# One tile of gathered and one of turned rows for all fours of experts, weights in two more places, and evictions put between the matmuls that turn the rows

## The chip, the core and the metric

The kernel runs on one core of one Trainium2 chip. The metric is the device time of one execution in microseconds (us), the median of several runs. The profile is of one execution. Engines are named as in the profile: PE is TensorE, DVE VectorE, ACT ScalarE, POOL GpSimd, SP SyncE, which issues the loads of weights.

## What is computed

Two transformer blocks over 512 tokens of width 1024, in float32. The change touches the last part of the second block alone, a mixture of 32 experts in four groups. Each token goes to two experts of one group. What has to come out is this sum, kept here in its plainest form:

```python
for e in range(N_EXPERTS):                       # 32 experts, w_gate and w_up 1024x256, w_down 256x1024
    act = jax.nn.silu(hf @ w_gate[e]) * (hf @ w_up[e])
    y = y + combine[:, e:e + 1] * (act @ w_down[e])
x = x + gate2 * y
```

The weights of the experts are 32 x 3 x 1 MB; every one of them has to be read once.

## The kernel before

Before the experts, the kernel writes the 512 rows of the block's input to a DRAM tile `h_d` and to the output, works out each token's experts, and sorts the tokens by expert (lines 1880 to 2060). An expert has 32 or more places for rows. The experts are worked in eight **fours**: the 128 rows of a four are 4 x 32 places, and a second set of 128 (`r` = 0 and 1) takes what the experts with many tokens have over.

For each four `q`:

- `rows_in(q)` **gathers** 2 x 128 rows from `h_d` into a tile `gb`, by two indirect DMAs on POOL.
- `turn(q, r, banks)` **turns** 128 rows: eight matmuls against a scaled unit matrix (`norm_of`, tile `dg`) put the 1024 columns of the rows on the partitions, into two PSUM banks; eight evictions, alternately ACT and DVE, write `xT[:, r]`.
- Twelve **jobs** of 1 MB of weights each: eight (`k` = 0 to 7) for the gate and up products, four (`k` = 8 to 11) for the down product. A job is two half jobs (`r` = 0, 1) of four matmuls of 128x32 with 512 columns. For `r` = 1 the weights are first copied to a tile `wd` in another order (`deal`, line 2197; half of it on DVE, half on ACT).
- `acts` and `acts_T` (activation and its transposes, line 2170), `halves` (the down product's eviction, times the token's weight, into `yo`, line 2211), `add_rows` (two **scatters** on POOL that add the rows to the output in DRAM, line 2177).

The jobs run in a fixed order: the first four's eight gate and up jobs, then for each next four its eight and then the four down jobs of the four before it; at the end the last four's down jobs. Every engine works through its instructions in the order in which this code issues them. `beside(q, k)` issues what is put beside job `k`: the turns of four `q + 1` behind jobs 4 and 6 of four `q`, and the gathers of four `q + 2` behind job 6. Two tiles `gb` and two tiles `xT` are used in turn (`q % 2`).

Weights come through a ring of places, each 1 MB: 3 `wr`, 3 `wq`, 10 `wb`. `st.fill()` issues a load on SP as soon as the order of the program has a free place, and `st.free` hands a place back behind each job. `st.left` = `EARLY` = 3 says that the first three `wb` places that become free are not loaded again: the second `gb`, the second `xT` and `yo` take their room. From then on 13 places are in use.

While the tokens are being sorted, `keep_busy(n)` puts `n` filler matmuls (128x512, line 1880) into PE's order.

Of the kernel before, what the change touches and what calls it, by code (L numbers as in the profile page):

```python
# [15 lines left out]
AF = mybir.ActivationFunctionType  # L16
OP = mybir.AluOpType
# [3 lines left out]
D = 1024  # L21
# [15 lines left out]
NQ = NE // 4  # L37
# [4 lines left out]
MORE0, EARLY = 7, 3  # L42
# [316 lines left out]
def tile_kernel(ctx: ExitStack, tc: tile.TileContext, ws, ada, c_d, hT_d, cst_d, seq_d, bd_d, wr_d, pos_d, out):  # L359
    nc = tc.nc  # L360
    V, S, G, PE = nc.vector, nc.scalar, nc.gpsimd, nc.tensor
# [11 lines left out]
    bank = [psum.tile([128, 512], FT, name=f"bank{i}") for i in range(8)]  # L373
    B = lambda shape, dt=FT, name="b": bpool.tile(shape, dt, name=name, tag="B")
# [177 lines left out]
    st = Stream(order)  # L552
# [251 lines left out]
    p = unitA(v_h, v_l, two_banks)  # L804
# [3 lines left out]
    vm = mpool.tile([16, 128], FT, name="vm", tag="vm", bufs=1)  # L808
# [92 lines left out]
    vfm = mpool.tile([16, 512], FT, name="vfm", tag="vfm", bufs=1)  # L901
# [975 lines left out]
    def keep_busy(n):  # L1877

        for _ in range(n):
            PE.matmul(bank[1], lhsT=ident, rhs=io, start=True, stop=True)  # L1880

    gb, xT, yo = [], [], []

    def rows_place():
        gb.append(B([128, 2, D], name="gb"))
        G.memset(gb[-1], 0.0)
        xT.append(B([128, 2, 8, 128], name="xT"))

    rows_place()


    sc, used = [], [0]
# [50 lines left out]
    V.tensor_tensor(oh, io9[:, None, None, :].to_broadcast([128, 2, 4, 32]),  # L1943
                    ek[:, :, :, None].to_broadcast([128, 2, 4, 32]), op=OP.is_equal)
    V.tensor_add(cnt_h, oh[:, 0], oh[:, 1])
    keep_busy(9)

    pt, before, placed = bank[0][:, :32], *(bank[0][:, 32 + 128 * j:160 + 128 * j].rearrange("p (i e) -> p i e", i=4)
                                            for j in range(2))
# [4 lines left out]
        for i in (3, 2, 1):  # L1954
            PE.matmul(ps[:, 4 - i:], lhsT=every, rhs=cnt_h[:, :i], start=False, stop=i == 1 and ps is before)
    PE.matmul(placed, lhsT=every, rhs=first_4, start=False, stop=True)
    keep_busy(8)
    V.tensor_sub(ex, m2, m1)

    def over(x):  # L1960
# [59 lines left out]
        hot(k)  # L2020
    inv = bank[2][:, :16]
    by_slot(inv, ohb, lambda n: tk[:, n, 0])
    keep_busy(2)
    hidx = cpool.tile([128, 16], I32, name="hidx")
    r4s, w_s = (cpool.tile([128, 16], FT, name=n) for n in ("r4s", "w_s"))
    V.tensor_scalar(hidx, inv, float(NONE), None, op0=OP.add)
# [7 lines left out]

    def rows_in(q):
        for r in range(2):
            gather(gb[q % 2][:, r], hidx[:, 2 * q + r:2 * q + r + 1])

    rows_in(0)
    st.hold, st.queue = False, G  # L2040
# [102 lines left out]
    def norm_of(scale, tag):  # L2143
        d = mpool.tile([128, 128], FT, name="dg", tag=tag, bufs=1)
        V.tensor_scalar(d, ident, scale, None, op0=OP.mult)
        return d

    def turned(x, g, d, banks):

        for h, p in enumerate(banks):  # L2150
            for t in range(4):
                PE.matmul(p[:, 128 * t:128 * t + 128], lhsT=g[:, 512 * h + 128 * t:512 * h + 128 * t + 128], rhs=d,
                          start=True, stop=True)
            for t in range(4):
                n, s = 4 * h + t, p[:, 128 * t:128 * t + 128]
                if t % 2:
                    V.tensor_scalar(x[:, n], s, a1[:, 8 + n:9 + n], MOD(3, n), op0=OP.mult, op1=OP.add)
                else:
                    S.activation(x[:, n], s, AF.Identity, bias=MOD(3, n), scale=a1[:, 8 + n:9 + n])

    def act(p):
        a = mpool.tile([128, 256], FT, name="ea", tag="cbm")
# [13 lines left out]
    def scatter(y, idx):  # L2176
        return G.indirect_dma_start(out=out[0], out_offset=bass.IndirectOffsetOnAxis(ap=idx, axis=0), in_=y,  # L2177
                                    in_offset=None, bounds_check=SEQ - 1, oob_is_err=False, compute_op=OP.add)

    def turn(q, r, banks):  # L2180
        turned(xT[q % 2][:, r], gb[q % 2][:, r], norm_of(r4s[:, 2 * q + r:2 * q + r + 1], "vfm" if r else "vm"), banks)

    def lot_regs(q):
        return [vload(lot_i[0:1, 4 * q + j:4 * q + j + 1], 1536, [ET.DVE if j < 2 else ET.Activation]) for j in range(4)]
# [21 lines left out]
    def own(w):  # L2206
        return lambda j: w[:, 512 * j:512 * j + 512]

    def halves(q, h):
        for r in range(2):  # L2210
            V.scalar_tensor_tensor(yo[0][:, r, 512 * h:512 * h + 512], bank[4 + 2 * h + r], w_s[:, 2 * q + r:2 * q + r + 1],
                                   gate[h], op0=OP.mult, op1=OP.mult)

    def add_rows(q):
        last = scatters[-1:]
        scatters[:] = [scatter(yo[0][:, r], hidx[:, 2 * q + r:2 * q + r + 1]) for r in range(2)]
        if q == NQ - 1:

            tc.declare_no_dep(scatters[1].ins, scatters[0].ins, reason="no row of out in both")
            tc.add_manual_dep(scatters[1].ins, last[0].ins.name,  # L2220
                              mybir.DependencyInfo(mybir.DependencyClass.Sync, mybir.DependencyReason.DATA),
                              reason="rows of out added to before")

    a, aT, scatters = {}, {}, []

# [8 lines left out]
    def beside(q, k):  # L2234

        other = bank[2 - 2 * (q % 2):4 - 2 * (q % 2)]
        aside[0] = other[1]
        if q and k == 0:
            acts(q - 1)
        elif q and k == 2:  # L2240
            acts_T(q - 1)
        elif k in (4, 6) and q + 1 < NQ:
            turn(q + 1, k // 2 - 2, other)
            if k == 6 and q + 2 < NQ:
                rows_in(q + 2)
        if q == 0 and k == 2:
            rows_place()
            rows_in(1)
            yo.append(B([128, 2, D], name="yo"))
            later.add(slot_weights())  # L2250
        elif q == 1 and k == 3:
            later.finish()
            later.add(crowded())
        elif q > 1 and k in (5, 7):
            later.tick()

    st.fill()
    st.left = EARLY
    turn0 = [norm_of(r4s[:, r:r + 1], "vfm" if r else "vm") for r in range(2)]
    dealt[0] = deal(0)  # L2260
    turned(xT[0][:, 0], gb[0][:, 0], turn0[0], bank[2:4])
    for i, (q, n) in enumerate(jobs):
        if i + 1 < len(jobs):
            dealt[i + 1] = deal(i + 1)
        w, t = dealt.pop(i)
        k = n - n_dense - 12 * q
        for r in range(2):
            if i == 0 and r == 1:
                turned(xT[0][:, 1], gb[0][:, 1], turn0[1], bank[4:6])
            if k < 8:  # L2270
                ps, x = bank[2 * (q % 2) + r], lambda c: xT[q % 2][:, r, k, c]
                first, last = k == 0, k == 7
            else:
                ps, x = bank[4 + 2 * (k // 10) + r], lambda c: aT[q][r][:, k % 2, c]
                first, last = k % 2 == 0, k % 2 == 1
            product(ps, x, (lambda j: t[:, j]) if r else own(w), first, last)
        st.free(("w", n))
        w = t = None
        st.fill()
        if k < 8:  # L2280
            beside(q, k)
        elif k == 10:
# [16 lines left out]
    with tc.For_i(0, n_any, 1) as _:  # L2299
        n_x = vload(nx_i[0:1, 0:1], NX)  # L2300
        with tc.For_i(0, n_x, 1) as i:
            raws = list(st.slots)[:3]
            vw = vload(ex_w[0:1, bass.ds(i, 1)], len(plan) - 12, [ET.SP])
            vj = vload(ex_j[0:1, bass.ds(i, 1)], 1536, [ET.SP])
            for c in range(3):
                for k in range(4):
                    nc.sync.dma_start(raws[c][:, 512 * k:512 * k + 512],
                                      ws[bass.ds(vw + (4 * c + k), 1), :, bass.ds(vj, 512)].rearrange("o p c -> p (o c)"))
            idx, sw = TN([128, 16], I32, name="idx")[:, :1], TN([128, 16], name="sw")[:, :2]
            V.tensor_copy(idx, hidx2[:, bass.ds(i, 1)])  # L2310
            V.tensor_copy(sw[:, :1], r4s2[:, bass.ds(i, 1)])
            V.tensor_copy(sw[:, 1:], w_s2[:, bass.ds(i, 1)])
            g, x, y = gb[0][:, 0], xT[0][:, 0], yo[0][:, 1]
# [38 lines left out]
```

## Time and profile before

| | us |
|---|---|
| median of 3 runs | 1619.85 (1619.43 to 1620.01) |
| the profiled execution | 1618.47 |
| its span, first to last instruction | 1616.7 |
| PE busy in the span | 1537.2 (95%) |
| DVE busy | 923.3 (57%) |
| ACT busy | 657.0 (41%) |
| POOL busy | 201.2 (12%) |

The page cuts the span into 40 slices of 40 us. The experts fill the last seven or so: there the DMA engines stand at nine tenths or more, at 388 to 404 GB/s, while PE's busy share, DVE's and ACT's are as in the stages before. A busy PE is not a PE at its peak: a matmul's time in the records overlaps the next one's. How long a group of matmuls holds PE is read from the starts of one group and the next.

### The profile page before, as it was taken

The page shows a single profiled execution, that of the slowest core. Times are in us where ns is not written, and L with a number is a line of the kernel's source. Part 1 is how long each engine was busy: PE and PEld are TensorE (multiplying, and loading weights), DVE is VectorE, ACT ScalarE, POOL GpSimd, SP SyncE. Part 2 cuts the span into 40 slices and gives each one's busy share as a digit, 9 for nine tenths or more (in the row PEclk, how much of TensorE's full clock was granted, in tenths as well). Part 3 has the DMA queues.
Part 4 walks back from the last instruction along what each step waited for, and adds up shares of the span by engine and source line. Part 5 has one row for each costly group of instructions (what it writes and reads, how often), then busy time and mean ns, then how long its engine had stood idle before and what let it go on. Part 6 is the DMA issues. An engine that isn't in the chain of part 4 may idle for free. (4 is left out here: it accounts for less than half of the span.)

```text
span 1616.7 us, 22593 instructions
## 1 busy us (share of the span) xinstructions
PE 1537.2 (95%) x8524; PEld 1153.4 (71%) x8524; DVE 923.3 (57%) x2020; ACT 657.0 (41%) x1208; POOL 201.2 (12%) x255
## 2 busy tenths in 40 slices
PE   7899999999999899999999999999999999998883
PEld 6788777788888778888889887778888874433321
DVE  5655455455757676664444755873466445565443
ACT  4445443326534332222233545653233215665442
POOL 0100111020030200000002142200013102111101
PEclk9999999999999999999999999999999999999997
DMA  5221221222235255445222241222223866999992
GB/s 187 92 79 67 92 80 53 79 91 79 103 137 215 104 209 208 181 186 193 105 83 100 79 143 54 78 79 85 95 82 134 312 234 258 388 404 392 395 390 65
DMA packets 49327, 258.28 MB, mean 160 GB/s; under 512 B 7316, under 2 KB 15636, under 8 KB 21184
## 3 DMA queue, kind: packets, MB, share of 16 engines
q1 hardware_dynamic: 41680, 237.17, 38.6%
q0 software_dynamic: 7248, 19.65, 4.2%
q8 instruction: 67, 1.10, 0.3%
q14 instruction: 44, 0.36, 0.1%
q10 hardware_dynamic: 288, 0.01, 0.0%
HBM read 250.48 MB, written 14.71 MB: 164 GB/s over the span
## 5 line engine op out<-in xcount | busy, mean ns | idle before, releaser
L493 DVE TENSOR_TENSOR wp<-wr,wp 128x1024 fp32r<-128x1024 f32 (+1 forms) x198 | 246.1, 1246 | 198.5 <-ACT wp L492 197.8
L492 ACT CAST wp<-wr 128x1024 fp32r<-128x1024 f32 (+1 forms) x198 | 204.2, 1035 | 111.3 <-PE bank L601 82.2
L599 PE MATMUL bank<-uh,wp 128*128 128x512 f32 (+1 forms) x464 | 150.7, 361 | 5.5 <-DVE ka L806 4.5
L601 PE MATMUL bank<-ul,wp 128*128 128x512 f32 (+1 forms) x464 | 144.4, 348 | 0.0
L603 PE MATMUL bank<-uh,wp 128*128 128x512 f32 (+1 forms) x464 | 144.1, 347 | 0.0
L599 PE MATMUL bank<-fh,wp 128*128 128x512 f32 x304 | 119.3, 392 | 6.6 <-ACT wp L492 6.6
L603 PE MATMUL bank<-fh,wp 128*128 128x512 f32 x304 | 119.2, 392 | 0.6 <-DVE wp L493 0.5
L601 PE MATMUL bank<-fl,wp 128*128 128x512 f32 x304 | 119.1, 392 | 0.4 <-POOL fl L1197 0.4
L599 PE MATMUL bank<-z,wp 128*128 128x512 f32 x264 | 108.4, 411 | 0.0
L603 PE MATMUL bank<-z,wp 128*128 128x512 f32 x264 | 103.3, 391 | 0.0
L601 PE MATMUL bank<-z,wp 128*128 128x512 f32 x264 | 102.9, 390 | 0.0
L599 PEld LDWEIGHTS bank<-uh,wp 128*128 128x128 f32 x464 | 81.0, 190 | 24.1 <-issue 6.8
L603 PEld LDWEIGHTS bank<-uh,wp 128*128 128x128 f32 x464 | 81.1, 190 | 11.2
L601 PEld LDWEIGHTS bank<-ul,wp 128*128 128x128 f32 x464 | 81.0, 190 | 9.8
L2197 ACT COPY wd<-wb 128x512 f32 x108 | 60.7, 616 | 55.9 <-DMA wb<-in_ws_dram 21.1
L2204 PE MATMUL bank<-wd,xT 128*32 128x512 f32 x512 | 78.5, 603 | 0.9 <-DVE wd L2197 0.6
L599 PE MATMUL bank<-ah,wp 128*128 128x512 f32 (+1 forms) x218 | 76.1, 349 | 0.0
L601 PE MATMUL bank<-al,wp 128*128 128x512 f32 (+1 forms) x218 | 75.9, 348 | 0.0
L603 PE MATMUL bank<-ah,wp 128*128 128x512 f32 (+1 forms) x218 | 75.9, 348 | 0.0
L599 PEld LDWEIGHTS bank<-fh,wp 128*128 128x128 f32 x304 | 57.6, 189 | 19.2 <-ACT wp L492 7.4
L603 PEld LDWEIGHTS bank<-fh,wp 128*128 128x128 f32 x304 | 57.4, 189 | 13.6 <-DVE wp L493 1.7
L601 PEld LDWEIGHTS bank<-fl,wp 128*128 128x128 f32 x304 | 57.5, 189 | 12.8 <-POOL fl L1197 0.8
(627 smaller groups left out, 3186.5 us busy)
## 6 DMA issues: line engine op xcount, KB each, us to landing
wr<-in_ws_dram SPq DMA_DIRECT2D x115, 1024.0 KB, 4.8
wb<-in_ws_dram SPq DMA_DIRECT2D x54, 1024.0 KB, 20.3
wr<-in_ada_dram SPq DMA_DIRECT2D x24, 1024.0 KB, 5.2
wq<-in_ws_dram SPq DMA_DIRECT2D x21, 1024.0 KB, 24.0
wr<-in_ws_dram SPq DMA_DIRECT2D x4, 768.0 KB, 4.2
ncb<-cum_d POOLq DMA_DIRECT2D x8, 264.0 KB, 3.7
wr<-in_ws_dram SPq DMA_DIRECT2D x4, 512.0 KB, 5.3
h_d<-row SPq DMA_DIRECT2D x8, 256.0 KB, 4.1
```

What stands on the lines that cost most here:

```text
L492: S.copy(h[:, :fl], t)
L493: eng.tensor_sub(l[:, :fl], t, h[:, :fl].bitcast(FT))
L599: PE.matmul(ps, lhsT=wh(k), rhs=rh(k, sl), start=first and k == 0, stop=False)
L601: PE.matmul(ps, lhsT=wh(k), rhs=rl(k, sl), start=False, stop=False)
L603: PE.matmul(ps, lhsT=wl(k), rhs=rh(k, sl), start=False, stop=last and k == nk - 1)
L2197: (V.tensor_copy if j < 2 else S.copy)(t[:, j], w[:, bass.ds(regs[q][j], 512)])
L2204: PE.matmul(ps[c], lhsT=x(c), rhs=w(j), start=first, stop=last)
```

## The change

- **One `gb` and one `xT`.** Both are made once, and `gb[q % 2]`, `xT[q % 2]` become `gb`, `xT`. With `st.left = 1`, set behind the fifth job, one place of the ring is given up, for `yo`; 15 remain in use.
- **Where turns and gathers stand.** The second four is turned behind job 7 of the first, both halves at once. From then on four `q + 2` is turned behind the down jobs 8 and 9 of four `q`, into the banks of four `q`'s own gate and up products, and four `q + 3` is gathered behind job 9. The gathers of the second four stand behind the first four's second turn.
- **How a turn is issued.** Before, the four matmuls of a bank and then its four evictions; after, each matmul and then its eviction.
- **The last four's rows** go to `gb` and not to `yo` (`rows_out`).
- **Scatters.** The second scatter of a four no longer waits for the first; both wait for both of the four before.
- **Fewer fillers:** 9, 8 and 2 become 5, 5 and 1 (a last 2 stays).

```diff
-    gb, xT, yo = [], [], []
-
-    def rows_place():
-        gb.append(B([128, 2, D], name="gb"))
-        G.memset(gb[-1], 0.0)
-        xT.append(B([128, 2, 8, 128], name="xT"))
-
-    rows_place()
+    gb, xT, yo = B([128, 2, D], name="gb"), B([128, 2, 8, 128], name="xT"), []
+    G.memset(gb, 0.0)
...
-    keep_busy(9)
+    keep_busy(5)
...
-    keep_busy(8)
+    keep_busy(5)
...
-    keep_busy(2)
+    keep_busy(1)
...
-        for h, p in enumerate(banks):
-            for t in range(4):
-                PE.matmul(p[:, 128 * t:128 * t + 128], lhsT=g[:, 512 * h + 128 * t:512 * h + 128 * t + 128], rhs=d,
-                          start=True, stop=True)
-            for t in range(4):
-                n, s = 4 * h + t, p[:, 128 * t:128 * t + 128]
-                if t % 2:
-                    V.tensor_scalar(x[:, n], s, a1[:, 8 + n:9 + n], MOD(3, n), op0=OP.mult, op1=OP.add)
-                else:
-                    S.activation(x[:, n], s, AF.Identity, bias=MOD(3, n), scale=a1[:, 8 + n:9 + n])
+        for n in range(8):
+            s = banks[n // 4][:, 128 * (n % 4):128 * (n % 4) + 128]
+            PE.matmul(s, lhsT=g[:, 128 * n:128 * n + 128], rhs=d, start=True, stop=True)
+            if n % 2:
+                V.tensor_scalar(x[:, n], s, a1[:, 8 + n:9 + n], MOD(3, n), op0=OP.mult, op1=OP.add)
+            else:
+                S.activation(x[:, n], s, AF.Identity, bias=MOD(3, n), scale=a1[:, 8 + n:9 + n])
...
+    def rows_out(q):
+        return gb if q == NQ - 1 else yo[0]
+
...
-        last = scatters[-1:]
-        scatters[:] = [scatter(yo[0][:, r], hidx[:, 2 * q + r:2 * q + r + 1]) for r in range(2)]
-        if q == NQ - 1:
+        last = scatters[-2:]
+        scatters.extend(scatter(rows_out(q)[:, r], hidx[:, 2 * q + r:2 * q + r + 1]) for r in range(2))
+        one, two = scatters[-2:]
+        if q:
...
-        elif k in (4, 6) and q + 1 < NQ:
-            turn(q + 1, k // 2 - 2, other)
-            if k == 6 and q + 2 < NQ:
-                rows_in(q + 2)
+        if q == 0 and k == 7:
+            for r in range(2):
+                turn(1, r, other)
+            rows_in(2)
...
-            rows_place()
-            rows_in(1)
-            yo.append(B([128, 2, D], name="yo"))
             later.add(slot_weights())
+        elif q == 0 and k == 4:
+            st.left = 1
...
-    st.left = EARLY
...
+                rows_in(1)
...
+        elif k < 10 and q + 2 < NQ:
+
+            turn(q + 2, k - 8, bank[2 * (q % 2):2 * (q % 2) + 2])
+            if k == 9 and q + 3 < NQ:
+                rows_in(q + 3)
```

PE's order around the first turn of the fourth four, before, with the semaphores that an instruction waits for (`bank_82` and `bank_83` are the two banks of the turn, `DMASW` is a gather's landing):

```order
L2204 MATMUL bank_81<-wd,xT 32x512 [waits Activation_49] x2
L2152 MATMUL bank_82<-dg,gb 128x128 [waits DMASW7_49,DVE_49]
L2152 MATMUL bank_82<-dg,gb 128x128 x3
L2152 MATMUL bank_83<-dg,gb 128x128 x4
L2204 MATMUL bank_80<-wq,xT 32x512 [waits DMAHW0_49]
```

The same turn in PE's order after:

```order
L2195 MATMUL bank_85<-wd,aT 32x512 [waits Activation_49] x2
L2146 MATMUL bank_82<-dg,gb 128x128 [waits DMASW7_49,DVE_49]
L2146 MATMUL bank_82<-dg,gb 128x128 [waits Activation_49]
L2146 MATMUL bank_82<-dg,gb 128x128 [waits DVE_49]
L2146 MATMUL bank_82<-dg,gb 128x128 [waits Activation_49]
L2146 MATMUL bank_83<-dg,gb 128x128
L2146 MATMUL bank_83<-dg,gb 128x128 [waits Activation_49]
L2146 MATMUL bank_83<-dg,gb 128x128 [waits DVE_49]
L2146 MATMUL bank_83<-dg,gb 128x128 [waits Activation_49]
L2195 MATMUL bank_84<-wb,aT 32x512 [waits DMAHW4_49]
```

The turn has moved from the gate and up jobs of the third four to the down jobs of the second, and six of its eight matmuls now have a wait for ACT or DVE in front of them.

POOL's order at the end before, the scatters of the last three fours (`DMASW` here is the landing of an earlier scatter or the room in its queue):

```order
L2177 DMA out_dram<-yo,hidx 512x1024 [waits DMASW3_49,DMASW2_49,DVE_49]
L2177 DMA out_dram<-yo,hidx 512x1024 [waits DMASW4_49,DMASW3_49,DVE_49]
L2177 DMA out_dram<-yo,hidx 512x1024 [waits DMASW4_49,DVE_49]
L2177 DMA out_dram<-yo,hidx 512x1024 [waits DMASW5_49,DVE_49]
L2177 DMA out_dram<-yo,hidx 512x1024 [waits DMASW7_49,DMASW6_49,DVE_49]
L2177 DMA out_dram<-yo,hidx 512x1024 [waits DMASW0_49,DVE_49]
```

And after:

```order
L2168 DMA out_dram<-yo,hidx 512x1024 [waits DMASW2_49,DMASW1_49,DVE_49]
L2168 DMA out_dram<-yo,hidx 512x1024 [waits DVE_49]
L2168 DMA out_dram<-yo,hidx 512x1024 [waits DMASW4_49,DMASW3_49,DVE_49]
L2168 DMA out_dram<-yo,hidx 512x1024 [waits DVE_49]
L2168 DMA out_dram<-gb,hidx 512x1024 [waits DMASW6_49,DMASW7_49,DMASW5_49,DVE_49]
L2168 DMA out_dram<-gb,hidx 512x1024 [waits DMASW0_49,DVE_49]
```

The second scatter of a four has lost its wait for the first, and the last four's scatters read `gb`.

## Rows read from the trace of the kernel before

**Rows 1.** Stretches: length, busy of PE PEld DVE ACT POOL, clock, DMA share, GB/s.

```profile
1338.00:1349.00 11.00, 10.64 (x92) 5.96 (x96) 7.35 (x23) 7.89 (x19) 4.00 (x3) 1.00 0.22 60
...
1360.00:1570.00 210.00, 187.32 (x1516) 73.57 (x1508) 118.32 (x313) 117.55 (x237) 29.65 (x21) 1.00 1.01 395
```

**Rows 2.** Timeline, late: start, us, engine, line, operation, tiles [idle <-what ended it].

```profile
1513.43 1.07 PE L2204 MATMUL bank<-wb,aT 128*32 128x512 f32 x8 [0.22 <-DMA wb<-in_ws_dram]
```

**Rows 3.** Timeline of SP, first reload of weights.

```profile
1349.23 7.87 SPq L443 DMA_DIRECT2D wb<-in_ws_dram  x4
```

**Rows 4.** Timeline around one turn.

```profile
1431.26 2.05 PE L2152 MATMUL bank<-dg,gb 128*128 128x128 f32 x16
...
1432.45 0.46 ACT L2159 ACTIVATE xT<-bank,mod,a 128x128 f32<-128x128 f32 x1 [1.56 <-PE bank L2152]
...
1432.95 0.41 DVE L2157 TENSOR_SCALAR xT<-bank,a,mod 128x128 f32<-128x128 f32 x1 [2.36 <-ACT xT L2159]
...
1433.24 1.06 PE L2204 MATMUL bank<-wq,xT 128*32 128x512 f32 x8
```

**Rows 5.** Lines of the turn: ns shortest/median/longest, first and last start.

```profile
L2152 PE MATMUL bank<-dg,gb x256: 275/275/377, 1338.1 to 1540.1; 128*128 128x128 f32 x128
...
L2157 DVE TENSOR_SCALAR xT<-bank,a,mod x64: 398/410/414, 1339.7 to 1542.3; 128x128 f32<-128x128 f32 x64
...
L2159 ACT ACTIVATE xT<-bank,mod,a x64: 447/457/460, 1339.2 to 1541.8; 128x128 f32<-128x128 f32 x64
```

**Rows 6.** Timeline of the transposes of one activation.

```profile
1426.42 0.44 PE L2170 MATMUL bank<-ident,ea 128*128 128x128 f32 x2
...
1426.89 0.37 ACT L2173 COPY aT<-bank 128x256 f32<-128x256 f32 x1 [0.91 <-PE bank L2170]
...
1427.32 0.44 PE L2170 MATMUL bank<-ident,ea 128*128 128x128 f32 x2 [0.46 <-ACT aT L2173]
```

**Rows 7.** Timeline of PE, two half jobs seven apart.

```profile
1449.15 1.04 PE L2204 MATMUL bank<-wb,aT 128*32 128x512 f32 x8
...
1455.16 1.04 PE L2204 MATMUL bank<-wd,xT 128*32 128x512 f32 x8
```

**Rows 8.** Timeline from the first fillers to the first turn.

```profile
1315.57 7.89 PE L1880 MATMUL bank<-mbig,ident 128*128 128x512 f32 x18
...
1320.12 0.29 DVE L1945 TENSOR_TENSOR cnt<-rs 128x128 fp32r<-128x128 f32 x1
...
1322.90 0.92 PE L1951 MATMUL bank<-cnt,marks 128*128 128x32 f32 x4
...
1328.57 1.50 DVE L1998 TENSOR_TENSOR ohb<-mbig,rs 128x512 fp32r<-128x512 f32 x2
...
1331.22 1.35 PE L2010 MATMUL bank<-tk,ohb 128*128 128x16 f32 x8
...
1333.70 1.14 POOL L2029 DMA_INDIRECT gb<-h_d,hidx  x1 [4.18 <-DMA wb<-in_ws_dram]
...
1338.07 2.02 PE L2152 MATMUL bank<-dg,gb 128*128 128x128 f32 x16 [1.06 <-DMA gb<-h_d,hidx]
```

**Rows 9.** Timeline of the end.

```profile
1593.30 1.39 PE L2204 MATMUL bank<-wd,aT 128*32 128x512 f32 x8
...
1600.10 2.07 DVE L2211 SCALAR_TENSOR_TENSOR yo<-bank,w_s,cst 128x512 f32<-128x512 f32 x3 [4.72 <-DMA out_dram<-yo,hidx]
...
1603.64 1.55 POOL L2177 DMA_INDIRECT out_dram<-yo,hidx  x1 [0.30 <-issue]
```

**Rows 10.** Stretches about two falls of the clock, and PE's first work after one.

```profile
899.00:903.00 4.00, 3.71 (x25) 3.04 (x24) 2.97 (x7) 2.62 (x5) 0.00 (x0) 0.96 0.00 0
...
903.00:906.00 3.00, 3.00 (x9) 2.35 (x8) 2.75 (x9) 1.02 (x2) 0.00 (x0) 0.50 0.59 142
...
1571.00:1575.00 4.00, 3.34 (x16) 0.86 (x20) 0.96 (x3) 1.35 (x3) 0.00 (x0) 0.58 0.96 375
...
1571.66 1.94 PE L2204 MATMUL bank<-wr,xT 128*32 128x512 f32 x8 [2.04 <-DMA wr<-in_ws_dram]
```

More of the change, by code (lines that the diff above doesn't have):

```diff
@@ L2036, in rows_in @@
         for r in range(2):
-            gather(gb[q % 2][:, r], hidx[:, 2 * q + r:2 * q + r + 1])
+            gather(gb[:, r], hidx[:, 2 * q + r:2 * q + r + 1])
     rows_in(0)
@@ L2180, in turn @@
     def turn(q, r, banks):
-        turned(xT[q % 2][:, r], gb[q % 2][:, r], norm_of(r4s[:, 2 * q + r:2 * q + r + 1], "vfm" if r else "vm"), banks)
+        turned(xT[:, r], gb[:, r], norm_of(r4s[:, 2 * q + r:2 * q + r + 1], "vfm" if r else "vm"), banks)
     def lot_regs(q):
@@ L2207, in own @@
         return lambda j: w[:, 512 * j:512 * j + 512]
+    def rows_out(q):
+        return gb if q == NQ - 1 else yo[0]
     def halves(q, h):
         for r in range(2):
-            V.scalar_tensor_tensor(yo[0][:, r, 512 * h:512 * h + 512], bank[4 + 2 * h + r], w_s[:, 2 * q + r:2 * q + r + 1],
-                                   gate[h], op0=OP.mult, op1=OP.mult)
+            V.scalar_tensor_tensor(rows_out(q)[:, r, 512 * h:512 * h + 512], bank[4 + 2 * h + r],
+                                   w_s[:, 2 * q + r:2 * q + r + 1], gate[h], op0=OP.mult, op1=OP.mult)
     def add_rows(q):
-        last = scatters[-1:]
-        scatters[:] = [scatter(yo[0][:, r], hidx[:, 2 * q + r:2 * q + r + 1]) for r in range(2)]
-        if q == NQ - 1:
[L2219 to L2222, printed above, removed]
+        last = scatters[-2:]
+        scatters.extend(scatter(rows_out(q)[:, r], hidx[:, 2 * q + r:2 * q + r + 1]) for r in range(2))
+        one, two = scatters[-2:]
+        if q:
+            tc.declare_no_dep(two.ins, one.ins, reason="no row of out in both")
+            for s in (one, two):
+                for t in last:
+                    tc.add_manual_dep(s.ins, t.ins.name,
+                                      mybir.DependencyInfo(mybir.DependencyClass.Sync, mybir.DependencyReason.DATA),
+                                      reason="rows of out added to earlier")
     a, aT, scatters = {}, {}, []
@@ L2257, in tile_kernel @@
     st.fill()
-    st.left = EARLY
     turn0 = [norm_of(r4s[:, r:r + 1], "vfm" if r else "vm") for r in range(2)]
     dealt[0] = deal(0)
-    turned(xT[0][:, 0], gb[0][:, 0], turn0[0], bank[2:4])
+    turned(xT[:, 0], gb[:, 0], turn0[0], bank[2:4])
     for i, (q, n) in enumerate(jobs):
@@ L2268, in tile_kernel @@
             if i == 0 and r == 1:
-                turned(xT[0][:, 1], gb[0][:, 1], turn0[1], bank[4:6])
+                turned(xT[:, 1], gb[:, 1], turn0[1], bank[4:6])
+                rows_in(1)
             if k < 8:
-                ps, x = bank[2 * (q % 2) + r], lambda c: xT[q % 2][:, r, k, c]
+                ps, x = bank[2 * (q % 2) + r], lambda c: xT[:, r, k, c]
                 first, last = k == 0, k == 7
@@ L2279, in tile_kernel @@
         st.fill()
+        if not st.left and not yo and i > 4:
+            yo.append(B([128, 2, D], name="yo"))
         if k < 8:
             beside(q, k)
-        elif k == 10:
+        elif k < 10 and q + 2 < NQ:
+            turn(q + 2, k - 8, bank[2 * (q % 2):2 * (q % 2) + 2])
+            if k == 9 and q + 3 < NQ:
+                rows_in(q + 3)
+        if k == 10:
             halves(q, 0)
@@ L2312, in tile_kernel @@
             V.tensor_copy(sw[:, 1:], w_s2[:, bass.ds(i, 1)])
-            g, x, y = gb[0][:, 0], xT[0][:, 0], yo[0][:, 1]
+            g, x, y = gb[:, 0], xT[:, 0], yo[0][:, 1]
             gather(g, idx)
```

## The prediction

> **What bounds the kernel now.** I read the table of stretches first, then the timeline of the last 300 us, then the groups of the lines that the change touches. The experts are the stage from 1338 us to the end. Between 1360 and 1570 us the 16 DMA engines are at 1.01 of their time and carry 395 GB/s, while TensorE is busy 187.32 of 210 us [rows 1]. Late in the stage a job begins when its 1 MB of weights lands: TensorE has waited for that DMA [rows 2]. At 395 GB/s a load of 1.049 MB takes 2.65 us, gathers and scatters between them counted. The first weights that go into a used place are issued at 1349.23 [rows 3]; before that the DMA engines are at 0.22 [rows 1]. So weights set the pace, and the last matmul ends at 1593.30 + 1.39 = 1594.69. Behind it VectorE waits until 1600.10 for a scatter of the seventh four, the last scatter is issued at 1603.64 [rows 9], and the span ends at 1616.7, 13.06 us later.
>
> TensorE has room, and how much decides this case. A product of one half job costs (1455.16 - 1449.15) / 7 = 0.859 us when nothing is waited for [rows 7]; 192 of them are 164.9 us. A turn of 128 gathered rows holds TensorE from 1431.26 to 1433.24, 1.98 us [rows 4]; 16 of them are 31.7. Eight pairs of transposes of the activations cost 1427.32 + 0.44 - 1426.42 = 1.34 each [rows 6], 10.7, and two sorts by slot 1.35 each [rows 8], 2.7. Together 210 us, against 1594.69 - 1338.07 = 256.6 that the stage takes: TensorE waits some 46 us in all.
>
> **The change part by part.** *The turn.* Before, four matmuls fill a bank back to back, then ScalarE and VectorE empty it while TensorE goes on with the next product. Now one matmul is followed by its own eviction, and the order shows what that means: of the eight matmuls of a turn, six wait for ScalarE or VectorE, all but the first of each bank. The waits follow the bank, not the 128 columns. The trace shows that this is how banks are shared here: ScalarE and VectorE, which read different columns of one bank, already take turns (ScalarE's first eviction starts at 1432.45 and takes 0.46, VectorE's at 1432.95, ended by ScalarE's) [rows 4, 5]. No row shows the new chain itself, so I build a step of it. A matmul is two records of 0.275 us [rows 5], begun (2.05 - 0.275) / 15 = 0.118 apart [rows 4], 0.39 us. The eviction is 0.457 on ScalarE, 0.410 on VectorE [rows 5]. The two hand-overs come from the nearest chain of this kind, transposes, ScalarE's copy, transposes: 1427.32 - 1426.42 = 0.90 less 0.44 and 0.37 leaves 0.09 [rows 6]. A step is 0.94 with ScalarE and 0.89 with VectorE; with hand-overs of 0.15, since ScalarE began 0.09 after the fourth matmul's end in [rows 4], it is 1.00 and 0.95. A turn has four steps with ScalarE, two with VectorE and two matmuls without a wait (0.24 each): 6.0 to 6.4 us, I take 6.2. That is 4.2 us more than 1.98, and nothing hides it on TensorE, which takes its work in order: the products behind the turn, and so the places that they free, wait.
>
> The row says that readers of one bank alternate; a rule fits beside it. The Trainium skill (PSUM — Partial Sum Buffer, PSUM bank collisions raise a hardware error) has engines kept apart by bank and by quarter of the partitions, and not by address. These tiles use all 128 partitions, so by that rule every matmul must wait as the order has it; by a rule that went by columns the turn would stay at 1.98 us.
>
> *Where it stands on the path.* Sum for TensorE with weights always there: 16 x 6.2 = 99.2, and 164.9 + 10.7 + 2.7, in all 277.5 us. That is more than the 256.6 that the weights allow now, so the bound moves from the weights to TensorE.
>
> *One tile of gathered and of turned rows, two more places.* The gathers of the next four wait for the turn that reads the same tile; they have some 20 us until they are needed, the cover being the products of a four. If that cover were gone a gather would cost what it does at the start, 1338.07 - 1333.70 = 4.4 us [rows 8]. The second four is turned behind the eighth job of the first, with nothing between: that is in the sum. Two places more let weights run 2 x 2.65 us further ahead; with TensorE as the bound they wait in their places, so I cost this at nothing, between -5 and 0. If the weights were the bound it would be worth those 5 us.
>
> *Fewer filler matmuls.* One is 7.89 / 9 = 0.88 us (two records each) [rows 8]. The count of experts is there at 1320.12 + 0.29 = 1320.41, TensorE comes to it at 1322.90; with five fillers instead of nine it is free at about 1320: 2.5 us. The second lot ran to 1331.22 while the one-hot rows were ready at 1328.57 + 1.50 = 1330.07: another 1.1 us or so, and half of that matmul group can start before the second one-hot tile: 0.5. The gather is thus issued about 4 us earlier, but weights are still landing then and share the engines. I take the first turn to start 3 us earlier, at 1335, between 1334 and 1338.07.
>
> *The end.* The last four's rows go to the row tile, so VectorE no longer waits for the seventh four's scatters [rows 9], and scatters run in pairs. After the last matmul there remain an eviction (2.07 / 3 = 0.69), one scatter's 1.55 on GpSimd [rows 9] and the wait for the seventh's pair, which goes out four jobs (4 x 2 x 0.859 = 6.9 us) less an eviction before: last issue 3.4 us after TensorE instead of 1603.64 - 1594.69 = 8.95; bounds 2.3 and 8.95.
>
> *Sum at full clock.* 1335 + 277.5 = 1612.5 for TensorE, + 3.4 + 13.06 = 1629 span. The profiled run took 1.77 us more than its span and lies 1.38 below the median: **1632**.
>
> **The clock.** In a turn TensorE now streams two short records in each microsecond and waits the rest. Rows show that the granted clock can fall for less than a stop: in 899 to 903 us TensorE is recorded busy 3.71 of 4 us, part of it one-column matmuls, and the next 3 us are granted 0.50 [rows 10]; between 1571 and 1575 the mean is 0.58, after a wait of 2.04 us [rows 10]. That is 1.2 instead of 2.4 GHz. The price: the first half product there took 1.94 us for 1.06 [rows 10], so a job loses 1.75. Two turns stand with one job between. If the clock falls inside each pair and stays low through the job, the second turn and some 4 us behind, a pair loses 1.75 + 1.5 (its eight matmuls at half rate, estimated from the doubling) + 2 = 5.2; if it falls once in each turn for the 3 to 4 us that it stayed low after 1571, 2 x 1.75 = 3.5. Eight pairs: 28 to 42 us, I take 40. Nearest row: 899 to 903, where TensorE is recorded busier (3.71 of 4 us) than a turn can keep it (0.39 of each 0.9 us), and the clock fell all the same. So I expect the fall: 1632 + 40 = **1672**.
>
> The Trainium skill (TensorE: Matmul & The Clock Gate, A second HAM failure mode: psum-queue depth-cycling) describes a kernel that cycles through PSUM, idles briefly between groups and swings between the two clocks. By it the time is the forecast's; no run yet shows it for this chain.
>
> **Rivals.** *The clock holds.* For it: between 1360 and 1570 the granted clock stayed 1.00 although TensorE waited over a tenth of the time [rows 1]. Against it: those waits are shorter than a whole turn. Time 1632 (1626 to 1644 by the bounds). *The weights stay the bound*, and the kernel gets faster: this happens if the turns fit in the slack, that is if a turn costs under (1593.30 - 1335 - 178.3) / 16 = 5.0 us, (5.0 - 2 x 0.24) / 6 = 0.75 a step. Then the tail gives 5.5 us, and an earlier first reuse, at about 1342 for 1349.23, up to 7: about 1611. Against it: matmul and eviction alone are 0.39 + 0.41 = 0.80. *It comes out even*: a turn near 5.3 us, TensorE as late as the weights were plus what the tail gave: 1617 to 1623. *More waits than I count*, evictions queued behind copies of weights that have not landed, each turn over 7.5 us with the clock low: above 1690.
>
> **How the numbers follow.** Clock falls 0.60 (1655 to 1690), clock holds 0.26, weights still the bound 0.06, even 0.04, above 1690 0.04. The range takes the first and the second, 1626 to 1690, and leaves 0.14 outside. About 0.2% is what a measurement of this kernel can tell from no change, 1616.6 to 1623.1: faster 0.07, same 0.03, slower 0.90.
>
> **What would show it.** Right: groups of matmuls of a turn with idle time before them ended by ScalarE and VectorE, some 6 us from the first to the last; TensorE's waits for weights gone and the DMA engines below 0.95 between 1360 and 1570; a new wait of the DMA queue for TensorE; slices of granted clock under 9 in the expert stage; the last scatter issued 3 to 4 us after the last matmul. Wrong: turns of 2 us, or a span under 1616 with weights landing to the end.

## The result, and the profile after

The changed kernel takes 1691.08 us (median of 4 runs, 1690.03 to 1692.2) against 1619.64 for the kernel before in the same comparison: the ratio is 1.0445, its 95% interval 1.0427 to 1.0463. It is 71 us slower. The forecast was slower, at 1672, with 1690 as the upper end of its range: the direction and the mechanism held, and the size fell short by 19 us, which is just past the upper end.

The stretches of the expert stage, answering to [rows 1] (length, busy PE PEld DVE ACT POOL, clock, DMA share, GB/s):

```profile
1338.00:1349.00 11.00, 7.80 (x24) 4.15 (x24) 2.31 (x6) 2.85 (x7) 0.99 (x1) 0.50 0.31 106
1349.00:1360.00 11.00, 9.26 (x42) 3.87 (x46) 2.47 (x7) 2.48 (x6) 0.99 (x1) 0.54 0.23 63
1360.00:1640.00 280.00, 230.90 (x1500) 88.24 (x1496) 119.54 (x317) 119.24 (x236) 30.14 (x26) 0.80 0.80 306
```

Before, TensorE was granted 1.00 here and the DMA engines were at 1.01. Now the clock's mean is 0.80 over 280 us and the DMA engines carry 306 GB/s at 0.80 of their time: the weights no longer set the pace. The queue that issues them says the same, in the table of waits (who waited for what: us in all, times, the longest):

```profile
SPq L443 <- PE bank L2195: 263.9, 80, 20.3
```

```profile
SPq L443 <- PE bank L2204: 57.9, 31, 3.4
```

The first row is the changed kernel's: all 80 loads into used places waited for TensorE to be done with a place, 263.9 us; in the kernel before (second row) 31 did, 57.9 us. So this wait is not new, as the prediction's sign has it; it has taken the place of the waits for weights. On the page, TensorE's clock and the DMA engines over the 40 slices of the span, and the group of the turn's matmuls (busy and mean ns of one, then the idle time ahead of them):

```profile
PEclk9999999999999999999999999999999768877888
DMA  5222121222354454552232412122256547888882
...
L2146 PE MATMUL bank<-dg,gb 128*128 128x128 f32 x256 | 79.1, 414 | 54.8 <-ACT xT L2150 35.1
```

ScalarE's evictions ended 35.1 us of TensorE's idle time ahead of these matmuls, and most of the rest was VectorE's. One turn on TensorE, in the down jobs of the second four, with the products on both sides of it (start, length, operation, idle time before and what ended it):

```profile
1408.66 0.49 PE L2146 MATMUL bank<-dg,gb 128*128 128x128 f32 x2
1409.70 0.49 PE L2146 MATMUL bank<-dg,gb 128*128 128x128 f32 x2 [0.55 <-ACT xT L2150]
1410.69 0.49 PE L2146 MATMUL bank<-dg,gb 128*128 128x128 f32 x2 [0.51 <-DVE xT L2148]
1411.73 0.71 PE L2146 MATMUL bank<-dg,gb 128*128 128x128 f32 x4 [0.55 <-ACT xT L2150]
1412.99 0.49 PE L2146 MATMUL bank<-dg,gb 128*128 128x128 f32 x2 [0.55 <-ACT xT L2150]
1413.98 0.80 PE L2146 MATMUL bank<-dg,gb 128*128 128x128 f32 x2 [0.50 <-DVE xT L2148]
1415.32 0.80 PE L2146 MATMUL bank<-dg,gb 128*128 128x128 f32 x2 [0.55 <-ACT xT L2150]
1416.05 1.94 PE L2195 MATMUL bank<-wb,aT 128*32 128x512 f32 x8
```

Before, the sixteen records of a turn stood in one row [rows 4]. Now each pair of records (one matmul) but the first stands alone behind an idle time of 0.50 to 0.55 us that ScalarE or VectorE ends; the row of four is two matmuls, the second in the fresh bank. From 1413.98 on a matmul takes 0.80 instead of 0.49 and the half product (the products of half a job) behind takes 1.94 instead of 1.04: the clock has fallen to half inside the turn. It was the same at the start of the stage, where TensorE had waited for the gather:

```profile
1334.48 0.46 PE L2146 MATMUL bank<-dg,gb 128*128 128x128 f32 x2 [2.03 <-DMA gb<-h_d,hidx]
...
1343.28 1.94 PE L2195 MATMUL bank<-wb,xT 128*32 128x512 f32 x8
```

The first turn began 3.6 us earlier than in [rows 8] and took 1343.28 - 1334.48 = 8.80 us. The end (PE, then the scatters on POOL):

```profile
1670.46 1.04 PE L2195 MATMUL bank<-wd,aT 128*32 128x512 f32 x8
...
1673.36 1.56 POOL L2168 DMA_INDIRECT out_dram<-gb,hidx  x1 [4.76 <-DMA out_dram<-yo,hidx]
1675.22 1.55 POOL L2168 DMA_INDIRECT out_dram<-gb,hidx  x1 [0.30 <-issue]
```

The last scatter is issued 1675.22 - 1671.50 = 3.7 us behind the last matmul, for 8.95 before [rows 9].

**Where the 71 us are.** From the first turn to the last matmul's end TensorE takes 1671.50 - 1334.48 = 337.0 us, for 256.6 before. The sixteen turns, each from its first matmul to the next product, add up to 130.0 (7.08 to 9.15 each; two stand together as 18.06 us, with one wait of 0.70 for the scaled unit matrix between them), for 31.7. Eight pairs of transposes take 1.27 each, two sorts 1.0 each, 12.2 in all; what is left for the products is 194.8, for 164.9. So turns +98.3, products at a lower clock +30, less the 46.6 us that TensorE had to spare, less 1.2: +80.5. The earlier first turn takes off 3.6 and the shorter end 5.2; 71.7 remain, and the spans differ by 1688.3 - 1616.7 = 71.6.

### The profile page after: what moved, and what is told of

It reads as the page before. It is cut to its first block, busy times and chain, and to the rows that moved or that the text cites. A ratio compares the mean times of both kernels' runs of the same rounds, so it can differ in the third digit from the quotient of the medians.

```text
span 1688.3 us, 22551 instructions
## 1 busy us (share of the span) xinstructions
PE 1582.9 (94%) x8508; PEld 1165.9 (69%) x8508; DVE 925.5 (55%) x2020; ACT 660.5 (39%) x1208; POOL 198.8 (12%) x254
## 5 line engine op out<-in xcount | busy, mean ns | idle before, releaser
L2146 PE MATMUL bank<-dg,gb 128*128 128x128 f32 x256 | 79.1, 414 | 54.8 <-ACT xT L2150 35.1
L2146 PEld LDWEIGHTS bank<-dg,gb 128*128 128x128 f32 x256 | 51.0, 256 | 96.8 <-ACT xT L2150 50.8
L2148 DVE TENSOR_SCALAR xT<-bank,a,mod 128x128 f32<-128x128 f32 x64 | 26.2, 410 | 129.5 <-PE bank L2146 129.5
L2188 ACT COPY wd<-wb 128x512 f32 x120 | 68.2, 617 | 55.0 <-PE bank L2195 37.6
L2150 ACT ACTIVATE xT<-bank,mod,a 128x128 f32<-128x128 f32 x64 | 29.3, 458 | 116.8 <-PE bank L2146 116.8
```

The source lines that it names most:

```text
L2146: PE.matmul(s, lhsT=g[:, 128 * n:128 * n + 128], rhs=d, start=True, stop=True)
L2188: (V.tensor_copy if j < 2 else S.copy)(t[:, j], w[:, bass.ds(regs[q][j], 512)])
```

## Experiments

The theory: the waits for evictions between the matmuls of a turn, and the clock that falls in them, are the whole loss. The rivals: turns side by side, late gathers and fewer fillers cost as well; the clock falls only where two turns stand close together; the waits go by something else than the bank. The ratios are to the kernel before, on the same chip in the same comparison, with 95% intervals.

**The old form of the turn in the changed kernel.**

```diff
-        for n in range(8):
-            s = banks[n // 4][:, 128 * (n % 4):128 * (n % 4) + 128]
-            PE.matmul(s, lhsT=g[:, 128 * n:128 * n + 128], rhs=d, start=True, stop=True)
...
+        for h, p in enumerate(banks):
+            for t in range(4):
+                PE.matmul(p[:, 128 * t:128 * t + 128], lhsT=g[:, 512 * h + 128 * t:512 * h + 128 * t + 128], rhs=d,
+                          start=True, stop=True)
+            for t in range(4):
+                n, s = 4 * h + t, p[:, 128 * t:128 * t + 128]
...
```

> The changed kernel with the turn alone put back to its old form: four matmuls of a bank, then its four evictions. Theory (the waits for evictions between the matmuls of a turn, and the clock that falls in them, are the whole loss): a turn holds TensorE 2 us again, the granted clock stays at 1.00 from 1360 us on, the weights set the pace again, and what is left of the change gains: the last scatter 5 us earlier and the first reuse of a place up to 7 us earlier, 1605 to 1614 us. Rival (two turns side by side, late gathers into one tile and fewer fillers cost as well): 1625 us or more, with TensorE waiting for gathers or with the clock low in the first turns.

Measured (the batched kernel): 1610.17 us, ratio 0.9952 (0.9935 to 0.9968). The stretch that answers to [rows 1]:

```profile
1360.00:1570.00 210.00, 188.24 (x1524) 72.30 (x1525) 119.25 (x316) 118.98 (x239) 31.10 (x23) 0.98 0.99 389
```

Two turns of a pair with what stands behind them on TensorE, the first load into a used place, and the end:

```profile
1412.95 2.05 PE L2146 MATMUL bank<-dg,gb 128*128 128x128 f32 x16 [0.47 <-DVE dg L2139]
1414.93 1.07 PE L2198 MATMUL bank<-wb,aT 128*32 128x512 f32 x8
...
1418.24 2.02 PE L2146 MATMUL bank<-dg,gb 128*128 128x128 f32 x16 [1.38 <-ACT wd L2191]
```

```profile
1341.63 9.47 SPq L443 DMA_DIRECT2D wb<-in_ws_dram  x5
```

```profile
1590.68 1.39 PE L2198 MATMUL bank<-wd,aT 128*32 128x512 f32 x8
...
1593.70 1.55 POOL L2171 DMA_INDIRECT out_dram<-gb,hidx  x1 [6.60 <-DVEq L2305]
1595.56 1.55 POOL L2171 DMA_INDIRECT out_dram<-gb,hidx  x1 [0.30 <-issue]
```

Turns of 2 us again, DMA engines at 0.99, and the end short. The granted clock is 0.98 and not the 1.00 of the theory; from 1360 us on one turn is partly at half clock, the second behind the first four's eighth job (1361.22), ahead of which TensorE waited 2.56 us for an eviction. One function's order is the whole loss, and the rest of the change gains: the first load into a used place is issued at 1341.63 instead of 1349.23 [rows 3], the last matmul ends at 1592.07 instead of 1594.69, and the last scatter comes 3.5 us behind it. TensorE waits for no gather but the first. The rival that puts a part of the loss on the other edits is out.

**The new form of the turn in the kernel before.** The same lines the other way, nothing else.

> The kernel before with only the new form of the turn: each matmul followed by its own eviction, all else as before. Theory: a turn costs what the trace of the changed kernel shows, 6.6 us at full clock and up to 9.1 at half, so TensorE becomes the bound: first turn 1338, products, transposes and sorts 177 us, 16 turns of some 8 us 128, products at half clock behind each turn 16 x 1.75 = 28, so last matmul near 1671, and with the old end 22 us behind it and 1.8 us around the span 1695 us; 1675 to 1705. Rival (the clock falls only because two turns stand close together; single turns keep it): 16 x 6.6 = 106 us of turns and no loss behind them, 1645 us. Rival (the loss comes from the other parts of the change): 1620 us.

Measured: 1696.81 us, ratio 1.0487 (1.0470 to 1.0505), within 2 us of the theory's sum. The stretch, and a turn behind the fifth job of a four, with the products of two jobs between it and the next turn:

```profile
1360.00:1600.00 240.00, 198.74 (x1284) 74.04 (x1280) 101.05 (x274) 101.57 (x201) 26.55 (x24) 0.81 0.77 293
```

```profile
1444.76 0.49 PE L2152 MATMUL bank<-dg,gb 128*128 128x128 f32 x2
...
1449.09 0.79 PE L2152 MATMUL bank<-dg,gb 128*128 128x128 f32 x2 [0.55 <-ACT xT L2156]
...
1452.45 1.94 PE L2201 MATMUL bank<-wq,xT 128*32 128x512 f32 x8
```

The clock falls in a single turn too, here from its sixth matmul on (1449.09), and the products behind it pay as in the changed kernel. The rival that needs two turns close together is out: here at least two jobs lie between turns from the second four on, and the granted clock is 0.81 all the same.

**Even matmuls into one bank, odd ones into the other.** The order of all instructions stays that of the changed kernel.

```diff
-            s = banks[n // 4][:, 128 * (n % 4):128 * (n % 4) + 128]
+            s = banks[n % 2][:, 128 * (n // 2):128 * (n // 2) + 128]
```

> The changed kernel with one index changed: matmul n of a turn goes to bank n modulo 2, not n divided by 4, so that a matmul and the eviction before it are in different banks; the order of the instructions stays. Theory (the wait goes by bank): a matmul waits for the eviction two before it, the two chains of four run side by side, a turn takes some 3.6 us at full clock, TensorE needs 1334.5 + 177 + 58 = 1570 us at full clock and is under the weights again even if the clock falls in some turns: 1605 to 1620 us. Rival (any order of one matmul and one eviction makes the clock fall as before, and with it the loss): turns of 5 us or more and half clock behind them, 16 x 5 + 30 + 177 + 1334.5 + 18.8 = 1640 us.

Measured: 1615.05 us, ratio 0.9981 (0.9971 to 0.9991). A turn on TensorE, to the product behind it:

```profile
1391.47 0.71 PE L2146 MATMUL bank<-dg,gb 128*128 128x128 f32 x4
1392.51 0.71 PE L2146 MATMUL bank<-dg,gb 128*128 128x128 f32 x4 [0.33 <-ACT xT L2150]
1393.55 0.71 PE L2146 MATMUL bank<-dg,gb 128*128 128x128 f32 x4 [0.33 <-ACT xT L2150]
1394.58 0.71 PE L2146 MATMUL bank<-dg,gb 128*128 128x128 f32 x4 [0.33 <-ACT xT L2150]
1395.22 1.06 PE L2195 MATMUL bank<-wb,aT 128*32 128x512 f32 x8
```

```profile
1360.00:1570.00 210.00, 185.88 (x1504) 72.39 (x1508) 120.63 (x317) 120.33 (x240) 32.29 (x24) 0.99 0.99 387
```

Two matmuls now go in each step of 1.04 us, and a turn takes 1395.22 - 1391.47 = 3.75 us for the 7.1 to 9.1 of the changed kernel. That is below the 5.0 us that the prediction has the weights allow; the stretch has the clock at 0.99 and the DMA engines at 0.99, so the weights set the pace again. The loss is gone but for some 5 us against the batched kernel. About half of that is there early: the seventh load into a used place is issued 2.4 us later than there (1358.37 for 1355.93). The rest was not followed up. The order of matmul and eviction was not the fault by itself; that a matmul follows the eviction of its own bank was. The waits stand in the program's order, which here has one wherever one engine follows another on a bank; a kernel without them was not tried. That fits the rule of the Trainium skill (PSUM — Partial Sum Buffer, PSUM bank collisions raise a hardware error) by which engines are kept apart by bank and not by column; no run here shows what happens without the wait.

**Fillers in the waits.** What does the clock cost by itself? The waits stay, and TensorE gets work in them (`keep` is true in every turn of the fours).

```diff
             PE.matmul(s, lhsT=g[:, 128 * n:128 * n + 128], rhs=d, start=True, stop=True)
+            if keep and n < 7:
+                PE.matmul(bank[7][:, 256:], lhsT=ident, rhs=io[:, :256], start=True, stop=True)
```

> The changed kernel with a filler matmul of 256 columns into another bank behind each of the first seven matmuls of a turn, so that TensorE has work while it waits for the eviction; the waits for evictions stay. It tells what the clock costs by itself. Theory (the clock falls because TensorE stands idle inside the turns, and costs about as much as the waits): granted clock near 1.00 from 1350 us on, turns of 6.6 to 7 us, 1334.5 + 177 + 16 x 6.9 = 1622, and 18.8 behind: 1638 to 1648 us. Rival (the clock falls for another reason, or costs little): 1690 us or more, clock as low as in the changed kernel.

Measured: 1652.2 us, ratio 1.0206 (1.0189 to 1.0223). The stretch, and of one turn the first matmul, its filler, the second and the last matmul and the product behind:

```profile
1360.00:1600.00 240.00, 227.42 (x1638) 96.00 (x1630) 113.41 (x301) 114.95 (x227) 29.17 (x23) 1.00 0.90 349
```

```profile
1399.75 0.49 PE L2146 MATMUL bank<-dg,gb 128*128 128x128 f32 x2
1400.08 0.60 PE L2148 MATMUL bank<-mbig,ident 128*128 128x256 f32 x2
1400.79 0.49 PE L2146 MATMUL bank<-dg,gb 128*128 128x128 f32 x2
...
1406.54 0.49 PE L2146 MATMUL bank<-dg,gb 128*128 128x128 f32 x2
1406.96 1.06 PE L2197 MATMUL bank<-wb,aT 128*32 128x512 f32 x8
```

The granted clock is 1.00 in this stretch, the links of the chain are as long as they were (1400.79 is 1.04 behind 1399.75), and 39 us are gone although TensorE has more to do. Only the first turn, behind a wait of 3.48 us for the gather, still ran in part at half clock. A turn takes 1406.96 - 1399.75 = 7.21 us. One filler per turn lies where there is no wait, behind the fourth matmul, and costs 0.43; without it the turn at full clock is 6.78. The time is 4 us above the expected range: the gather came 2.6 us later in this execution (first turn at 1337.10), the turns took 7.3 on average with the first at 8.1 and not 6.9, and the products 4.6 more than at full pace. As a price of the clock: the 39 us, the fillers' own 16 x 0.43 = 6.9 and the later gather's 2.6 make some 48. The turns and products of the changed kernel add up to 51 (next section).

The same with fillers of half the size:

```diff
-                PE.matmul(bank[7][:, 256:], lhsT=ident, rhs=io[:, :256], start=True, stop=True)
+                PE.matmul(bank[7][:, 384:], lhsT=ident, rhs=io[:, :128], start=True, stop=True)
```

> As the filled kernel (1652 us), but fillers of 128 columns instead of 256, so that TensorE has half as much extra work in each wait. Theory (any work in the waits holds the clock, and the rest of the filled kernel's time over 1636 is the fillers' own): turns of 6.9 us at full clock, 1335 to 1337 + 177 + 16 x 6.9 + 18.8: 1641 to 1647 us. Rival (so little work is not enough, the clock falls in some turns as in the changed kernel): 1655 to 1690 us, with slices of granted clock under 9.

Measured: 1656.29 us, ratio 1.0231 (1.0215 to 1.0246), 9 us above the theory and at the low end of the rival. The two turns in which the clock was low, by their first matmuls:

```profile
1335.62 0.46 PE L2146 MATMUL bank<-dg,gb 128*128 128x128 f32 x2 [3.50 <-DMA gb<-h_d,hidx]
...
1374.53 0.80 PE L2146 MATMUL bank<-dg,gb 128*128 128x128 f32 x2 [0.70 <-DVE dg L2139]
```

Before the first, TensorE had waited 3.50 us for the gather; the other is the second turn of the pair behind the eighth job, ahead of which TensorE had waited 0.70 for the scaled unit matrix. These two turns took 9.2 and 9.5 us. The other fourteen kept the clock and took 7.0 to 7.1 (one of them with the 0.70 of that wait behind it): 6.78 and a filler of 0.22 that nothing hides. So half the work held the clock in fourteen turns of sixteen. That the longer waits ahead of the other two were the reason is not shown: a turn behind a wait of 0.55 us kept the clock here, and in the filled kernel with 256 columns the turn behind the same wait of 0.70 kept it too.

**The gain, by parts.** The batched kernel is 8 us faster than the kernel before. The end alone, put into the kernel before: `add_rows` as in the change, and

```diff
+    def rows_out(q):
+        return gb[q % 2] if q == NQ - 1 else yo[0]
...
-            V.scalar_tensor_tensor(yo[0][:, r, 512 * h:512 * h + 512], bank[4 + 2 * h + r], w_s[:, 2 * q + r:2 * q + r + 1],
+            V.scalar_tensor_tensor(rows_out(q)[:, r, 512 * h:512 * h + 512], bank[4 + 2 * h + r], w_s[:, 2 * q + r:2 * q + r + 1],
```

> The kernel before with the end of the change alone: the last four's rows go to the row tile and the scatters of a four run side by side; turns, places, gathers and fillers as before. Theory (the end is worth the wait that it takes away, and nothing else): the last scatter is issued some 3.4 us after the last matmul instead of 8.95, so 5.5 us less: 1612 to 1615 us. Rival (scatters side by side get in the way of weights, or the wait comes back elsewhere): 1617 us or more.

Measured: 1614.0 us, ratio 0.9971 (0.9960 to 0.9983), 5.1 us less. Its end, last matmuls and last scatter:

```profile
1594.38 1.39 PE L2204 MATMUL bank<-wd,aT 128*32 128x512 f32 x8
...
1599.25 1.55 POOL L2177 DMA_INDIRECT out_dram<-gb,hidx  x1 [0.30 <-issue]
```

From the last matmul's end at 1595.77 to the last scatter's issue it is 3.5 us for 8.95, and that end is no earlier than before (1594.69), so the gain is the end's alone.

The fillers and the places, each put back in the batched kernel:

```diff
-    keep_busy(5)
+    keep_busy(9)
...
-    keep_busy(5)
+    keep_busy(8)
...
-    keep_busy(1)
+    keep_busy(2)
```

> The batched kernel (the changed one with the old form of the turn, 1610.2 us) with the old numbers of filler matmuls, 9, 8 and 2 for 5, 5 and 1. Theory (fewer fillers give nothing, as the first turn waits for its gather anyway): within 2 us of the batched kernel, 1608 to 1612, the first turn at full clock. Rival (the 3 us that the prediction put on fewer fillers are real): 1613 us or more. Rival (the low clock of the first turns costs): 1607 us or less.

Measured: 1611.31 us, ratio 0.9953 (0.9939 to 0.9967), the batched kernel's time. The first turn here and in the batched kernel, with the product behind it:

```profile
1340.48 2.02 PE L2146 MATMUL bank<-dg,gb 128*128 128x128 f32 x16 [1.51 <-DVE wd L2191]
1342.43 1.06 PE L2198 MATMUL bank<-wb,xT 128*32 128x512 f32 x8
```

```profile
1337.09 2.56 PE L2146 MATMUL bank<-dg,gb 128*128 128x128 f32 x16 [2.06 <-DMA gb<-h_d,hidx]
1339.58 1.94 PE L2198 MATMUL bank<-wb,xT 128*32 128x512 f32 x8
```

It starts 3.4 us later and runs at full clock, 1.95 us to the product for 2.49. The 3 us are there, and where the weights set the pace no gain from them shows.

```diff
-            st.left = 1
+            st.left = 3
```

> The batched kernel with three places of the ring given up instead of one, so 13 in use as before the change. Theory (two more places are worth what they let weights run ahead, at most 2 x 2.65 us, where the weights set the pace): 1611 to 1616 us. Rival (the places give nothing, since a place is freed in time anyway): within 1 us of the batched kernel.

Measured: 1614.2 us, ratio 0.9969 (0.9958 to 0.9980), 4 us above the batched kernel by the medians, 3 by the ratios, whose intervals overlap, so the step is near the noise. The stretch in which the ring first runs short, here and in the batched kernel:

```profile
1360.00:1400.00 40.00, 36.01 (x292) 15.76 (x292) 22.30 (x65) 23.65 (x49) 4.80 (x5) 0.96 0.87 331
```

```profile
1360.00:1400.00 40.00, 36.65 (x297) 15.52 (x300) 22.83 (x66) 24.12 (x49) 4.58 (x4) 0.96 0.93 375
```

With 13 places the DMA engines are at 0.87 of these 40 us, with 15 at 0.93: 0.06 x 40 = 2.4 us of weights. End and places, 5 and some 3, make up the 8.

**A version that beats both.** In the batched form ScalarE and VectorE evict from one bank in turn. With even matmuls in one bank and odd ones in the other, all eight matmuls first, each engine has a bank:

```diff
+        s = [banks[n % 2][:, 128 * (n // 2):128 * (n // 2) + 128] for n in range(8)]
+        for n in range(8):
+            PE.matmul(s[n], lhsT=g[:, 128 * n:128 * n + 128], rhs=d, start=True, stop=True)
+        for n in range(8):
+            if n % 2:
+                V.tensor_scalar(x[:, n], s[n], a1[:, 8 + n:9 + n], MOD(3, n), op0=OP.mult, op1=OP.add)
+            else:
+                S.activation(x[:, n], s[n], AF.Identity, bias=MOD(3, n), scale=a1[:, 8 + n:9 + n])
```

> The batched kernel with the eight matmuls of a turn one behind the other, even ones into one bank and odd ones into the other, and then the evictions: ScalarE has a bank to itself and VectorE the other. Theory (two engines in one bank take turns; in two banks they go side by side): the evictions of a turn take 4 x 0.46 = 1.8 us instead of some 3.5, the second turn of the first pair no longer waits 2.6 us, and places come free up to 2 us earlier: 1606 to 1610 us. Rival (weights set the pace so that nothing of it is seen): the batched kernel's time within 1 us. Rival (evictions that start later, behind all eight matmuls, hold up the next product): 1612 us or more.

Measured (the split kernel): 1609.97 us, ratio 0.9941 (0.9927 to 0.9955). The evictions of one turn here, and the first of one in the batched kernel:

```profile
1410.25 1.50 ACT L2151 ACTIVATE xT<-bank,mod,a 128x128 f32<-128x128 f32 x4 [2.82 <-PE bank L2146]
...
1410.47 1.36 DVE L2149 TENSOR_SCALAR xT<-bank,a,mod 128x128 f32<-128x128 f32 x4 [2.15 <-PE bank L2146]
```

```profile
1414.15 0.46 ACT L2153 ACTIVATE xT<-bank,mod,a 128x128 f32<-128x128 f32 x1 [2.14 <-PE bank L2146]
1414.64 0.41 DVE L2151 TENSOR_SCALAR xT<-bank,a,mod 128x128 f32<-128x128 f32 x1 [1.74 <-ACT xT L2153]
...
1415.08 0.81 ACT L2153 ACTIVATE xT<-bank,mod,a 128x128 f32<-128x128 f32 x2 [0.48 <-DVE xT L2151]
```

Four evictions of each engine are done in 1.58 us, side by side, where in one bank an engine's eviction begins after the other's. It does not show in the time, as the rival had it: the evictions were not on the path.

And one line more:

```diff
-                turn(1, r, other)
+                turn(1, r, bank[2 + 2 * r:4 + 2 * r])
```

> The split kernel (1610.0 us) with the two turns behind the eighth job in banks of their own, so that the second needs no eviction of the first. Theory (TensorE's wait of 1.7 us there holds up the first places to be loaded again): 1607 to 1609 us. Rival (the weights make up for it, since TensorE has slack later): 1609 to 1611 us, as the split kernel.

Measured: 1607.39 us, ratio 0.9927 (0.9914 to 0.9941), the fastest kernel of the study, 0.7% below the kernel before. Its advantage over the split kernel is inside the two intervals. The edit did not take away the wait that it aimed at: TensorE's 1.70 us ahead of the second turn, ended by ScalarE's eviction, became 1.65, ended by VectorE's scaled unit matrix. What went is a wait of 1.37 us behind that turn. So what the wait is worth stays open.

## Why the prediction was right in kind and short in size

- *The weights bound the kernel before.* Right: with turns of 2 us and with turns of 3.75 us the time comes out under the old one, and the batched kernel's 1610 is the 1611 that the rival of that name gave for turns that fit in the slack. Of its parts, the end gave 5.1 for 5.5, and the first reuse is 7.6 us earlier for up to 7, of which 2.6 reach the last matmul.
- *Six of eight matmuls wait, and TensorE becomes the bound.* Right in mechanism, as the old turn put back alone and the new turn put in alone show, 1610.17 and 1696.81. **The size of a step was taken too small.** I took 0.94 to 1.00 with ScalarE and 0.89 to 0.95 with VectorE; the rows have 1.04 and 0.99. The hand-over was as estimated, 0.55 of idle time less 0.457 of eviction, 0.09. But a matmul alone takes 0.49 to its end (0.39 taken, from records in an unbroken row). With 0.42 instead of 0.24 behind the last one, a turn at full clock is 6.78 us and not 6.2: 16 x 0.58 = 9.3 us.
- *The clock falls in the turns.* Right, and fillers show its price apart from the waits. **This term was the one most short**: 40 taken, 51.4 measured. The products' part was right: 194.8 - 164.9 = 29.9, for 8 x 3.75 = 30. The turns' part was not: 130.0 - 16 x 6.78 = 21.5 (0.7 of it the wait for the scaled unit matrix), where I had 8 x 1.5 = 12. I had put half rate on the second turn of a pair alone, and priced it at 0.19 for each of eight matmuls, less than even their spacing of 0.24 in an unbroken row. In the rows the clock falls within the first turn of a pair already, and a step at half clock is 1.34 and 1.30 for 1.04 and 0.99: 0.31 more, which is what a matmul alone takes longer to its end, 0.80 for 0.49. I also rounded 41.6 down to 40. The Trainium skill (TensorE: Matmul & The Clock Gate, A second HAM failure mode: psum-queue depth-cycling) tells of such a swing between the two clocks; this trace agrees, with 0.80 as the mean and both rates within one turn.
- *Fewer fillers, 3 us.* The first turn began 3.6 us earlier. But TensorE then waited 2.03 us for the gather where it had waited 1.06 [rows 8], and the first turns and the half product between them ran mostly at half clock. Little of that belongs to this edit: the kernel before with the new turn and the old fillers had the same there, 8.49 for 8.80 in the first turn and 1.87 for 1.86 in the half product. Where the weights set the pace, no gain from the edit shows.
- *Two places more, at nothing with TensorE as the bound, up to 5 us otherwise.* In the changed kernel every load waits for TensorE; in the batched one they are worth some 3 us, near the noise. *Gathers into one tile, covered.* Right: TensorE waits for none but the first. *The end, 3.4 us behind the last matmul.* 3.7 measured, and 5.1 us gained by the end alone for 5.5.
- *The sum.* Turns at full clock +9.3, the clock +11.4, the earlier start -0.5, transposes and sorts -1.2, the end +0.3: 19.3 of the 19.1 us missing. The upper end of the range came from 42 us for the clock; that bound and the term itself rested on one price for half rate, so the range had no room for that price to be wrong.

## What to carry to other kernels

A loop that evicts each matmul before the next one into the same bank turns a run of matmuls into a chain, here 1 us a link for 0.24 us of work; issue the matmuls of a bank together, or let neighbours go to different banks. Such a chain costs twice: the waits (16 x 4.8 = 77 us here) and the clock that falls in them (51 us), at half rate within the chain and for some us of good work behind it. When a chain is priced at half clock, look for a matmul that stands alone at that clock and take its time to its end (here 0.80 for 0.49), not the spacing in a full row, and charge it from the first turn on.

## What the runs showed of the hardware that I had not expected

- Evictions of ScalarE and VectorE out of two banks run side by side, four each of 128x128 in 1.50 and 1.36 us; out of one bank in this program they alternate at 0.93 us a pair.
- The clock could be held by work of no use: with fillers of 256 columns in the waits it was 1.00 from 1360 us on, though in part low in the first turn, behind a wait of 3.48 us; with 128 columns it fell in two of sixteen turns, behind waits of 3.50 and 0.70 us.
- In the turn shown, TensorE fell to half clock after idle times of 0.50 to 0.55 us, none of them longer, between matmuls of 0.49 us each. With matmuls in pairs and idle times of 0.33 us, in two banks in turn, the clock was 0.99 from 1360 to 1570 us.
